# Normalising the last expert group in one batch, and the last expert's rows from its accumulators

## The chip, the cores and the metric

The kernel runs on one core of a Trainium2 chip. The core has a matrix engine (TensorE, PE in the rows, with its weight loads as PEld), a vector engine (VectorE, DVE), an activation engine (ScalarE, ACT), a general engine (GpSimd, POOL), and a queue that issues plain transfers (SyncE, SP). Every engine runs its own list of instructions in order and waits on semaphores for the others. The metric is the device time of one execution in microseconds (us). All times below are us unless ns is written.

## What is computed

One layer of a streaming encoder: two sequence mixers, a projection, and a mixture of experts, over 2048 tokens of 1024 numbers. The change is at the end, in the mixture and the last normalisation:

```python
def hier_moe(h, wg, bg, we, be, w_gate, w_up, w_down):
    """Top-1 expert group, then top-2 experts within it; gate = p(group) * softmax(top-2 logits)."""
    ...
    hg = lax.ragged_dot(xs, w_gate.astype(xs.dtype), sizes)
    hu = lax.ragged_dot(xs, w_up.astype(xs.dtype), sizes)
    ys = lax.ragged_dot(jax.nn.silu(hg) * hu, w_down.astype(xs.dtype), sizes)
    ys = ys * gates.reshape(-1)[order][:, None].astype(ys.dtype)
    y = jax.ops.segment_sum(ys, tok, num_segments=t)
    ...
        x = x + hier_moe(h2, router_g_w[layer], router_g_b[layer], router_e_w[layer], router_e_b[layer],
                         exp_w_gate[layer], exp_w_up[layer], exp_w_down[layer])
    return rmsnorm(x, norm_f_w)
```

There are 32 experts in 4 groups of 8. A token goes to one group and to two experts of it, so once the 8 experts of a group are done, the rows of all the group's tokens are final and can be normalised.

## The kernel before

The sequence mixers and the router run first, in four blocks of 512 tokens. They leave three things in device memory: the normalised tokens `x1d`, the residual rows `accd`, and lists `lst` of token numbers for each expert and each group, with their lengths in `cnt`. Then comes the expert stage, which this study is about.

**One expert.** Its tokens are gathered by number into `xg0` (the first 128) and `xg1` (those above 128, if any; when there are at most 64 of these, a form with half the rows is used, named `_half`). They are transposed on PE (`turn`) into a high part `xh` and a low part `xl`; weights are split in the same way, by a copy on ACT (`hi`, in the function `piece`) and a subtraction on DVE (`lo`). Products are summed in the accumulators `pg` and `pu` (gate and up), `act` makes the hidden rows `h` from them (Silu on ACT, a product on DVE; the half form ends with a product on POOL), `h` is transposed, and the down products land in two accumulators `pyd`, one for each half of the columns. They are copied out to `pv0` or `pv1`, and an indirect transfer adds these rows into `accd` (`puti`). Weights arrive in pieces of 512 KB into six buffers `mraw` (pool `wr_`), in the order that `stream` yields.

**The order of the work.** In this stage every engine's list is in the order in which the code is written. A string of letters sets it: step i runs through `ORDER`, each letter calls one part, and a dot feeds one more weight piece. A, B, C, D are the up products of expert i (A and C for the first 128 tokens, B and D for the rest); a and b are `act` for the two; X and Y transpose the next expert's tokens; H, K, d, e, g are the transposes of `h` and the down products of expert i-1; P and Q are its two transfers into `accd`; E and F load lists and gather tokens for expert i+2. So the down products of expert i-1 run inside step i, between its up products.

**The end of a group.** `group` assigns to each of the steps after a group's last expert a round q of that group: r (`group_count`) loads the numbers of 256 tokens into `fen` and gathers their rows from `accd` into the two tiles `f0` and `f1`, s (`group_norm`) squares and sums on ACT and takes the inverse root on POOL, m (`group_out`) scales on DVE and writes the rows to the output by number. A round is left out on the chip by a branch when the group has no tokens for it; the branch is taken on each engine, and POOL then advances the transfers' semaphores by hand. The first three groups' rounds lie inside the steps of later experts. The last group has no later experts: after step 32 its eight rounds follow one after another, lines 945 to 948.

**After the stage** comes a branch (line 952) around a slow path for lists that are too long, which these inputs don't take.

Of the kernel before, what the change touches and what calls it, by code (L numbers as in the profile page):

```python
# [38 lines left out]

ORDER = '.A.EB.HKC..r.Xa..D.b.dYePFsg..Qm'  # L40
FIRST, START = 5, 10
WB = 5
# [7 lines left out]
def hybrid_block_kernel(ctx, tc, x, norm1_w, w_in, ssd_conv_w, ssd_conv_b, ssd_dt_bias, ssd_a_log,  # L50
# [68 lines left out]

    cnt = consts.tile([1, 2 * NL + 1], I32, name="cnt")  # L120

# [336 lines left out]
    def route(b, r):  # L458
# [77 lines left out]
        if b == nblk - 1:  # L536
            pc = sc([1, NL], "pcnt")
            PE.matmul(pc, ones[:, 0:1], ohs, start=True, stop=True)
            V.tensor_scalar(cnt[:, 0:NL], pc, 63.0, None, op0=OP.add)
            V.tensor_scalar(cnt[:, NL:2 * NL], pc, 127.0, None, op0=OP.add)  # L540
            V.tensor_reduce(cnt[:, 2 * NL:], cnt[:, NL:NL + NE], axis=mybir.AxisListType.X, op=OP.max)
            V.tensor_scalar(cnt[:, 0:NL], cnt[:, 0:NL], 6, None, op0=OP.arith_shift_right)
            V.tensor_scalar(cnt[:, NL:], cnt[:, NL:], 7, None, op0=OP.arith_shift_right)
        return (last, lexp), en, sl

# [37 lines left out]
    def moe(x1, rs):  # L583

        me = ExitStack()
        wr_ = me.enter_context(tc.tile_pool(name="m_raw", bufs=RAW, reuse_waits="tile"))
# [145 lines left out]

        def down(t, h, w, n):
# [12 lines left out]

        def norm(r, sq):

            v = mp.tile([128, 2], F32, name="v")
            V.tensor_scalar(v, sq, 1.0 / D, EPS, op0=OP.mult, op1=OP.add)  # L752
            whole(rsqrt_steps(mp, r, v, 2, True))

# [86 lines left out]

        def scale_rows(t):
            V.scalar_tensor_tensor(fs[t], fs[t], r[:, t:t + 1], nf, op0=OP.mult, op1=OP.mult)

        def group_out(g, q):
            with tc.If(ngs[g] > 2 * q):
                for t in range(2):
                    scale_rows(t)
                    d = G.indirect_dma_start(out=out, out_offset=bass.IndirectOffsetOnAxis(ap=fen[t][:, 0:1], axis=0),  # L849
                                             in_=fs[t], in_offset=None, bounds_check=S - 1, oob_is_err=False)  # L850
                    apart(d, outs)
                    outs.append(d)
# [7 lines left out]
        def group_count(i):  # L860
# [4 lines left out]
            group_rows(g, q)  # L865

        def parts(i):

# [4 lines left out]
            w, wd = [], []  # L873
            fin = 0 <= group(i)[0] < NG - 1

# [28 lines left out]
            def downer(n):  # L904
                wd.extend(pull_down())
                down(0, ht[j][0], wd[4 * n:], n)

            def down_second():
                def full():
                    for n in range(2):  # L910
                        down(1, ht[j][1], wd[4 * n:4 * n + 4], n)

                def half():
                    for n in range(2):
                        down_half(ht[j][1], wd[4 * n:4 * n + 4], n)
                whole_or_half(j, full, half)

            def put1():
# [12 lines left out]
                P=(late, lambda: puti(j, 0)), Q=(late, put1), r=(fin, lambda: group_count(i)),  # L931
                s=(fin, lambda: group_norm(*group(i))), m=(fin, lambda: group_out(*group(i))))
# [12 lines left out]
        for i in range(NE + 2, NE + 2 + GE):  # L945
            group_count(i)
            group_norm(*group(i))
            group_out(*group(i))
        order.close()

        nmax = nc.values_load(cnt[0:1, 2 * NL:2 * NL + 1], min_val=0, max_val=S // 128)
        with tc.If(nmax > 2):
            for e in range(NE):
# [16 lines left out]
            with tc.For_i(0, S // 128, 1) as t:  # L970
                nc.sync.dma_start(fs[0], accd[bass.ds(t * 128, 128), :])
                square(fs[0], sq[:, 0:1])
                norm(r, sq)
                scale_rows(0)
                nc.sync.dma_start(out[bass.ds(t * 128, 128), :], fs[0])
# [326 lines left out]
```

## Time and profile before

| | us |
|---|---|
| median of 3 runs | 3080.14 |
| lowest and highest | 3077.07, 3081.48 |
| the profiled execution, its own time | 3078.34 |
| its span, first to last instruction | 3076.6 |
| TensorE busy | 2815.0 |
| VectorE busy | 2123.6 |
| ScalarE busy | 1485.0 |
| GpSimd busy | 692.5 |

The profile gives each engine's busy time in the span; a busy TensorE is not one at its peak. The span leaves out 1.74 us of the execution's own time, which lie around it. The granted clock is the share of TensorE's full clock that the chip allowed, 0.5 or 1.0 of it, averaged over a stretch.

### The profile page before, as it was taken

Reading aid. Unit: us, or ns where it says so; the run is one execution under the profiler, and the core shown is the slowest. Engines: PE = TensorE matmul, PEld = TensorE weight load, DVE = VectorE, ACT = ScalarE, POOL = GpSimd, SP = SyncE. Lnnn points to the kernel's source line nnn. Section 1 sums busy time; section 2 is a strip of 40 time slices with the busy share of each in tenths; the row PEclk is TensorE's granted clock in tenths of the full one; section 3 lists DMA queues with packets and bytes.
Section 4 is the critical chain, followed back from the end, with each engine's and each line's share of the span. In section 5 each row is a group of like instructions: output and inputs, shape, how many; then the busy total and the mean of one; then the engine's idle time right before and its main releaser. Section 6 shows DMA issues by size and latency. Waiting matters only on the chain. (4 is left out here: it accounts for less than half of the span.)

```text
span 3076.6 us, 41788 instructions
## 1 busy us (share of the span) xinstructions
PE 2815.0 (91%) x13412; PEld 2213.9 (72%) x13412; DVE 2123.6 (69%) x3969; ACT 1485.0 (48%) x2323; POOL 692.5 (23%) x770
## 2 busy tenths in 40 slices
PE   7999999999999999999999999984999899999870
PEld 6778877777877777887777788773667677777650
DVE  6896486788567679647768864855877777667741
ACT  5444345445434454434445443434666666556630
POOL 1421010451000064001025210013113323313412
PEclk9999999999999999999999999996999999999995
DMA  4222222422322241332233232145998998878951
GB/s 155 59 75 91 76 83 76 152 62 72 100 83 69 75 146 55 96 96 75 64 113 107 69 92 79 50 151 198 308 323 270 294 307 285 257 241 268 320 143 55
DMA packets 234320, 437.55 MB, mean 142 GB/s; under 512 B 43796, under 2 KB 43872, under 8 KB 234032
## 3 DMA queue, kind: packets, MB, share of 16 engines
q1 hardware_dynamic: 212064, 381.01, 38.0%
q0 software_dynamic: 21968, 53.02, 6.6%
q8 instruction: 142, 2.33, 0.3%
q14 instruction: 146, 1.20, 0.1%
HBM read 399.92 MB, written 54.98 MB: 148 GB/s over the span
## 5 line engine op out<-in xcount | busy, mean ns | idle before, releaser
L599 DVE TENSOR_TENSOR lo<-mraw,hi 128x1024 fp32r<-128x1024 f32 x384 | 456.4, 1231 | 79.3 <-ACT hi L598 64.4
L231 ACT ACTIVATE whi<-raw,pcol 128x512 fp32r<-128x512 f32 x416 | 294.9, 721 | 346.4 <-PE acc L269 143.0
L232 DVE SCALAR_TENSOR_TENSOR wlo<-raw,pcol,whi 128x512 fp32r<-128x512 f32 x416 | 317.9, 779 | 200.2 <-ACT whi L231 199.6
L598 ACT CAST hi<-mraw 128x1024 fp32r<-128x1024 f32 x384 | 384.1, 1051 | 87.0 <-DMA mraw<-in_exp_w_up_dram 39.1
L267 PE MATMUL acc<-hh,whi 128*128 128x512 f32 x896 | 366.8, 410 | 1.1 <-ACT whi L231 1.1
L267 PE MATMUL acc<-hh,wlo 128*128 128x512 f32 x896 | 358.1, 401 | 7.4 <-DVE wlo L232 7.4
L267 PE MATMUL acc<-hl,whi 128*128 128x512 f32 x896 | 361.0, 403 | 0.0
L269 PE MATMUL acc<-whi,hh 128*128 128x512 f32 x768 | 310.7, 405 | 2.0 <-ACT craw L280 2.0
L269 PE MATMUL acc<-whi,hl 128*128 128x512 f32 x768 | 310.8, 405 | 0.0
L269 PE MATMUL acc<-wlo,hh 128*128 128x512 f32 x768 | 309.4, 405 | 0.0
L269 PE MATMUL acc<-whi,mh 128*128 128x512 f32 x512 | 204.5, 399 | 0.0
L267 PEld LDWEIGHTS acc<-hh,wlo 128*128 128x128 f32 x896 | 169.3, 189 | 47.6 <-DVE wlo L232 9.8
L269 PE MATMUL acc<-whi,ml 128*128 128x512 f32 x512 | 203.5, 397 | 0.0
L269 PE MATMUL acc<-wlo,mh 128*128 128x512 f32 x512 | 203.2, 398 | 0.0
L281 POOL COPY hist<-craw 128x3 f32<-128x3 f32 x112 | 40.2, 359 | 723.7 <-ACT craw L280 723.3
L267 PEld LDWEIGHTS acc<-hh,whi 128*128 128x128 f32 x896 | 170.0, 190 | 34.4 <-issue 3.1
L267 PEld LDWEIGHTS acc<-hl,whi 128*128 128x128 f32 x896 | 169.8, 190 | 34.1 <-issue 4.6
L279 POOL COPY craw<-hist 128x3 f32<-128x3 f32 x112 | 71.0, 637 | 481.6 <-DVE ir L418 363.7
L269 PEld LDWEIGHTS acc<-wlo,hh 128*128 128x128 f32 x768 | 145.9, 190 | 36.6 <-issue 3.9
L269 PEld LDWEIGHTS acc<-whi,hh 128*128 128x128 f32 x768 | 146.1, 190 | 35.3 <-ACT craw L280 3.8
L269 PEld LDWEIGHTS acc<-whi,hl 128*128 128x128 f32 x768 | 146.1, 190 | 32.6 <-issue 1.9
L756 POOL DMA_INDIRECT accd<-pv,en x48 | 89.2, 1858 | 355.0 <-ACT hi L598 108.4
(379 smaller groups left out, 6143.6 us busy)
## 6 DMA issues: line engine op xcount, KB each, us to landing
raw<-in_w_in_dram SPq DMA_DIRECT2D x208, 512.0 KB
mraw<-in_exp_w_gate_dram SPq DMA_DIRECT2D x128, 512.0 KB
mraw<-in_exp_w_up_dram SPq DMA_DIRECT2D x128, 512.0 KB
mraw<-in_exp_w_down_dram SPq DMA_DIRECT2D x128, 512.0 KB
raw<-in_w_out_dram SPq DMA_DIRECT2D x64, 512.0 KB
xi<-in_x_dram SPq DMA_DIRECT2D x16, 512.0 KB
x<-in_x_dram SPq DMA_DIRECT2D x4, 2048.0 KB
accd<-x SPq DMA_DIRECT2D x16, 512.0 KB
```

Of the source, the lines that this page charges most:

```text
L231: A.activation(hi, src, AF.Copy, scale=w)
L232: V.scalar_tensor_tensor(lo, src, w, hi.bitcast(F32), op0=OP.mult, op1=OP.subtract)
L267: mm = PE.matmul(acc[i], b[:, s], a, start=f, stop=e)
L269: mm = PE.matmul(acc[i], a[:, s], b, start=f, stop=e)
L279: G.tensor_copy(raw[:, 0:3], hist[:, ct, :])
L281: h = G.tensor_copy(hist[:, ct, :], raw[:, T:T + 3])
L598: A.copy(hi, raw)
L599: V.tensor_tensor(lo, raw, hi.bitcast(F32), op=OP.subtract)
L756: return G.indirect_dma_start(out=accd, out_offset=bass.IndirectOffsetOnAxis(ap=en[:, 0:1], axis=0), in_=pvs[t], in_offset=None, bounds_ch ...
```

## The change

- The last two steps have strings of their own, `LAST`. In step 31, expert 30's down products come first and expert 31's up products behind them; `stream` yields the weights in that order.
- The last group is no longer handled in rounds behind step 32. In step 31, behind expert 30's transfers into `accd`, t (`last_rows`) gathers the group's first two tiles of rows and the rows of expert 31's own tokens (into `xg0` and `xg1`, which are free by then); u (`last_norm`) gathers four more tiles into weight buffers, squares all six on ACT, and takes the inverse roots of all six in one run of small instructions on DVE. In step 32, v, w and x scale two tiles each and write them out.
- Expert 31's rows no longer go through `accd`: `down` and `down_half` add the gathered rows when they empty the accumulators, and p and q (`expert_out`) square, normalise, scale and write these rows. Each write that may hit a row that an earlier one wrote waits for it.
- Rounds 4 to 7 of the first three groups are no longer there, not even as branches. Longer lists are left to the slow path, whose condition covers them.

```diff
 ORDER = '.A.EB.HKC..r.Xa..D.b.dYePFsg..Qm'
+LAST = '.H.Kd.e.PgQ.tA..B..C..ua.D.b', 'HvKwdepxgq'
+NQ = 4
...
             for i, e in enumerate(seq):
+                if i == NE - 2:
+                    yield from down_pieces(e)
+                    yield from up_pieces(seq[i + 1])
+                    continue
...
-        def down_half(h, w, n):
+        def down_half(h, w, n, g=None):
...
             A.copy(pv, pys[n][64:128])
+            if g is not None:
+                V.tensor_tensor(pv, pv, g[0:64, n * T:n * T + T], op=OP.add)
             V.tensor_tensor(pv, pys[n][0:64], pv, op=OP.add)
...
-            if n == 0:
+            if g is not None:
+                V.tensor_tensor(pv, pys[n], g[:, n * T:n * T + T], op=OP.add)
+            elif n == 0:
                 A.copy(pv, pys[n])
...
+        def last_rows():
+            for t in range(2):
+                fl.append(fs[t])
+                last_gather(fl[t], enl[:, t, :])
+            for t in range(2):
+                gt.append(xgs[t])
+                last_gather(gt[t], ens[NE - 1][t])
+
+        def last_norm():
+            assert next(rest, None) is None
+            n = 2 * NQ - 2
+            for t in range(2, n):
+                fl.append(wr_.tile([128, D], F32, name="mraw", tag="mraw"))
+                last_gather(fl[t], enl[:, t, :])
+            for t in range(n):
+                square(fl[t], sql[:, t:t + 1])
+            norm(rl[:, 0:n], sql[:, 0:n], False)
+
+        def last_out(ts):
+            for t in ts:
+                scale_rows(fl[t], fl[t], rl[:, t:t + 1])
+                d = to_out(fl[t], enl[:, t, 0:1])
+                apart(d, outs)
+                outs.append(d)
...
+        def expert_out(t):
+
+            square(pvs[t], sq[:, t:t + 1])
+            norm(r[:, t:t + 1], sq[:, t:t + 1], False)
+            scale_rows(gt[t], pvs[t], r[:, t:t + 1])
+            to_out(gt[t], ens[NE - 1][t][:, 0:1])
...
-            fin = 0 <= group(i)[0] < NG - 1
+            fin = 0 <= group(i)[0] < NG - 1 and group(i)[1] < NQ
+            rows = (lambda t: gt[t]) if j == NE - 1 else lambda t: None
...
-            for c in ORDER:
+            if i == NE - 2:
+                last_entries()
+            for c in ORDER if i < NE - 1 else LAST[i - NE + 1]:
...
-        for i in range(NE + 2, NE + 2 + GE):
-            group_count(i)
-            group_norm(*group(i))
-            group_out(*group(i))
...
-        nmax = nc.values_load(cnt[0:1, 2 * NL:2 * NL + 1], min_val=0, max_val=S // 128)
-        with tc.If(nmax > 2):
+        more_flag = nc.values_load(cnt[0:1, 2 * NL + 1:2 * NL + 2], min_val=0, max_val=S // 128 + 2 * NQ)
+        with tc.If(more_flag > 2 * NQ):
```

**ScalarE in step 31, around `act` of expert 31.** Before, the Silu that writes `h` from `pg` stands behind the last weight copies:

```order
L598 CAST hi<-mraw 128x1024 x2
L830 COMPARE_AND_BRANCH
L830 UNCONDITIONAL_BRANCH x2
L598 CAST hi<-mraw 128x1024
L732 ACTIVATE h<-pg_18244,en 128x512
L877 COMPARE_AND_BRANCH
```

and with the change:

```order
L606 CAST hi<-mraw 128x1024 x2
L962 COMPARE_AND_BRANCH
L963 COMPARE_AND_BRANCH
L963 UNCONDITIONAL_BRANCH x2
L962 UNCONDITIONAL_BRANCH
L763 ACTIVATE o,sql<-f_18244 128x1024
L763 ACTIVATE o,sql<-f_18245 128x1024
L763 ACTIVATE o,sql<-mraw 128x1024 x4
L746 ACTIVATE h<-pg_18246,en 128x512
```

The six squares now stand ahead of that Silu on its engine.

**GpSimd, from the last transfers into `accd` that the gathers wait for.** Before, that is behind expert 31 (line 663 is the gather, 837 opens `group_norm`):

```order
L863 TENSOR_LOAD cnt
L830 COMPARE_AND_BRANCH
L663 DMA f_18242<-accd,fen_31921 128x1024
L663 DMA f_18243<-accd,fen_31923 128x1024
L830 UNCONDITIONAL_BRANCH
L830 ISA
L830 UNCONDITIONAL_BRANCH
L837 COMPARE_AND_BRANCH
```

and with the change, behind expert 30 (line 675 is the gather):

```order
L675 DMA f_18244<-accd,enl 128x1024
L675 DMA f_18245<-accd,enl 128x1024
L675 DMA xg_18240<-accd,en 128x1024
L675 DMA xg_18241<-accd,en 128x1024
L962 COMPARE_AND_BRANCH
L963 COMPARE_AND_BRANCH
L963 UNCONDITIONAL_BRANCH x2
L962 UNCONDITIONAL_BRANCH
L675 DMA mraw<-accd,enl 128x1024 x4
```

Eight gathers follow one another with only the branch of B between them; before, each pair stood in a round with its norm and its writes behind it.

**VectorE in step 32, from the low part of `h`** (`hl`) **on.** Before (line 743 copies an accumulator out; 752 and 186 belong to a round):

```order
L229 TENSOR_TENSOR hl<-mt,hh 128x512
L877 COMPARE_AND_BRANCH
L878 COMPARE_AND_BRANCH
L229 TENSOR_TENSOR hh<-mt,hh 128x4x64
L878 UNCONDITIONAL_BRANCH
L229 TENSOR_TENSOR hl<-mt,hh 128x512
L878 UNCONDITIONAL_BRANCH
L877 UNCONDITIONAL_BRANCH
L830 COMPARE_AND_BRANCH
L830 UNCONDITIONAL_BRANCH x2
L743 COPY pv_18240<-pyd_18249 128x512
```

and with the change:

```order
L232 TENSOR_TENSOR hl<-mt,hh 128x512
L860 SCALAR_TENSOR_TENSOR f_18244<-f_18244,rl,nf 128x1024
L860 SCALAR_TENSOR_TENSOR f_18245<-f_18245,rl,nf 128x1024
L962 COMPARE_AND_BRANCH
L963 COMPARE_AND_BRANCH
L232 TENSOR_TENSOR hh<-mt,hh 128x4x64
L963 UNCONDITIONAL_BRANCH
L232 TENSOR_TENSOR hl<-mt,hh 128x512
L963 UNCONDITIONAL_BRANCH
L962 UNCONDITIONAL_BRANCH
L860 SCALAR_TENSOR_TENSOR mraw<-mraw,rl,nf 128x1024 x2
L755 TENSOR_TENSOR pv_18242<-pyd_18250,xg_18240 128x512
```

Four scalings of group rows now stand between the low part of `h` and the first emptied accumulator, and the emptying is an addition on VectorE where ScalarE copied.

## Rows read from the trace of the kernel before

**Rows 1.** Stretches: start:end, us; busy per engine (count); granted clock, DMA share, GB/s.

```profile
2600.00:2700.00 100.00, 99.33 (x464) 77.01 (x462) 67.92 (x76) 57.65 (x79) 28.34 (x30) 1.00 0.87 275
2986.00:3077.00 91.00, 0.00 (x0) 0.00 (x0) 9.14 (x13) 7.33 (x13) 23.24 (x49) 0.52 0.22 62
```

**Rows 2.** Timeline, all engines, from the last product: start, length, engine, line, instruction.

```profile
2985.42 0.40 PE L698 MATMUL pyd<-hi,hh 128*128 128x512 f32 x1
...
2988.00 1.56 POOL L756 DMA_INDIRECT accd<-pv,en  x1 [2.81 <-DVEq L846]
...
2995.18 1.06 POOL L663 DMA_INDIRECT f<-accd,fen  x1 [5.62 <-issue]
2996.55 1.02 POOL L663 DMA_INDIRECT f<-accd,fen  x1 [0.30 <-issue]
3000.36 1.06 ACT L747 ACTIVATE o<-f 128x1024 f32<-128x1024 f32 x1 [13.93 <-DMA f<-accd,fen]
...
3006.87 2.48 DVE L843 SCALAR_TENSOR_TENSOR f<-f,r,nf 128x1024 f32<-128x1024 f32 x2 [3.42 <-POOL r L195]
3008.43 1.83 POOL L849 DMA_INDIRECT out_dram<-f,fen  x1 [1.60 <-DVE f L843]
...
3013.56 1.04 POOL L663 DMA_INDIRECT f<-accd,fen  x1 [1.98 <-DMA out_dram<-f,fen]
...
3046.96 1.00 POOL L849 DMA_INDIRECT out_dram<-f,fen  x1 [0.31 <-DVEq L846]
```

**Rows 3.** GpSimd's queue at the end, by line: count, ns, first and last start.

```profile
L846 POOLq INC_SWDGE_SEM  x2: 1487/1489/1491, 3060.0 to 3063.8; - x2
...
L951 POOLq TENSOR_LOAD <-cnt x1: 310/310/310, 3065.3 to 3065.3; - x1
```

**Rows 4.** Timeline of TensorE in steps 31 and 32: A, d, H, d again.

```profile
2945.04 0.50 PE L686 MATMUL pg<-hi,xh 128*128 128x512 f32 x1 [0.73 <-ACT hi L598]
...
2964.80 0.40 PE L686 MATMUL pyd<-hi,hh 128*128 128x512 f32 x1
...
2974.11 0.60 PE L676 MATMUL mt<-ident,h 128*128 128x128 f32 x4
...
2976.51 0.50 PE L686 MATMUL pyd<-hi,hl 128*128 128x512 f32 x1 [0.45 <-DVE hl L229]
```

**Rows 5.** Timeline of VectorE in step 31.

```profile
2945.58 2.36 DVE L599 TENSOR_TENSOR lo<-mraw,hi 128x1024 fp32r<-128x1024 f32 x2 [0.53 <-DVEq L877]
2948.17 3.50 DVE L599 TENSOR_TENSOR lo<-mraw,hi 128x1024 fp32r<-128x1024 f32 x3 [0.23 <-DVEq L846]
2955.71 0.69 DVE L229 TENSOR_TENSOR hl<-mt,hh 128x512 fp32r<-128x512 f32 x1 [4.05 <-ACT hh L228]
...
2961.36 0.75 DVE L733 SCALAR_TENSOR_TENSOR h<-pu,en,h 128x512 f32<-128x512 f32 x1 [0.92 <-ACT h L732]
2965.19 0.68 DVE L711 TENSOR_TENSOR h<-pg,h 64x512 f32<-64x512 f32 x1 [3.09 <-ACT h L709]
```

**Rows 6.** Timeline of GpSimd in step 31: the last product of the half form.

```profile
2966.78 1.28 POOL L714 TENSOR_TENSOR h<-u,h 64x512 f32<-64x512 f32 x1 [18.52 <-ACT h L713]
```

**Rows 7.** Timeline of VectorE in a mixer stage: the inverse root's small instructions.

```profile
398.11 0.17 DVE L198 TENSOR_TENSOR rs_t<-rs_i 128x16 f32<-128x16 f32 x1
398.31 0.17 DVE L200 SCALAR_TENSOR_TENSOR rs_t<-rs_t,va 128x16 f32<-128x16 f32 x1
```

**Rows 8.** Timeline of TensorE in step 29, after an idle stretch.

```profile
2903.81 1.97 PE L676 MATMUL mt<-ident,xg 128*128 128x128 f32 x8 [4.35 <-DVE hl L229]
...
2907.67 0.63 PE L686 MATMUL pyd<-hi,hh 128*128 128x512 f32 x1
...
2908.60 0.40 PE L686 MATMUL pyd<-hi,hh 128*128 128x512 f32 x1
```

**Rows 9.** DMA issues by line: count, median us to landing.

```profile
accd<-pv,en POOLq DMA_INDIRECT x3, 8.9
...
out_dram<-f,fen POOLq DMA_INDIRECT x6, 3.4
```

More of the change, by code (lines that the diff above doesn't have):

```diff
@@ L118, in hybrid_block_kernel @@
     V.memset(ohs, 0.0)
-    cnt = consts.tile([1, 2 * NL + 1], I32, name="cnt")
+    cnt = consts.tile([1, 2 * NL + 2], I32, name="cnt")
     pcol = consts.tile([128, 172], F32, name="pcol")
@@ L733, in act, with down @@
             V.scalar_tensor_tensor(h, pas[t][1], ef[:, 4:5], h, op0=OP.mult, op1=OP.mult)
-        def down(t, h, w, n):
+        def down(t, h, w, n, g=None):
             for f, ww in enumerate(w):
@@ L747, in square, with norm @@
             A.activation(o, f, AF.Square, accum_out=sq)
-        def norm(r, sq):
-            v = mp.tile([128, 2], F32, name="v")
+        def norm(r, sq, pool_engine=True):
+            n = sq.shape[1]
+            v = mp.tile([128, n], F32, name="v%d" % n)
             V.tensor_scalar(v, sq, 1.0 / D, EPS, op0=OP.mult, op1=OP.add)
-            whole(rsqrt_steps(mp, r, v, 2, True))
+            whole(rsqrt_steps(mp, r, v, n, pool_engine))
         def add(t, en):
@@ L840, in group_norm, with scale_rows, to_out @@
                 norm(r, sq)
-        def scale_rows(t):
-            V.scalar_tensor_tensor(fs[t], fs[t], r[:, t:t + 1], nf, op0=OP.mult, op1=OP.mult)
+        def scale_rows(o, f, r):
+            V.scalar_tensor_tensor(o, f, r, nf, op0=OP.mult, op1=OP.mult)
+        def to_out(f, at):
+            return G.indirect_dma_start(out=out, out_offset=bass.IndirectOffsetOnAxis(ap=at, axis=0),
+                                        in_=f, in_offset=None, bounds_check=S - 1, oob_is_err=False)
         def group_out(g, q):
@@ L847, in group_out @@
                 for t in range(2):
-                    scale_rows(t)
-                    d = G.indirect_dma_start(out=out, out_offset=bass.IndirectOffsetOnAxis(ap=fen[t][:, 0:1], axis=0),
-                                             in_=fs[t], in_offset=None, bounds_check=S - 1, oob_is_err=False)
+                    scale_rows(fs[t], fs[t], r[:, t:t + 1])
+                    d = to_out(fs[t], fen[t][:, 0:1])
                     apart(d, outs)
@@ L865, in group_count, with last_entries, last_gather, last_more @@
             group_rows(g, q)
+        gl = NG - 1
+        sql, rl = (mp.tile([128, 2 * NQ], F32, name=n, bufs=1) for n in ("sql", "rl"))
+        enl = mp.tile([128, 2 * NQ, 8], I32, name="enl", bufs=1)
+        fl, gt = [], []
+        def last_entries():
+            at = (NE + gl) * S
+            after(nc.sync.dma_start(enl, lst[at:at + 2 * NQ * 128, :].rearrange("(t p) w -> p t w", p=128)), scat)
+        def last_gather(dst, at):
+            d = gather(dst, accd, at)
+            apart(d, [o for j, o in puts if j // GE != gl])
+        def last_rows():
[20 more added lines that the diff above has]
+                outs.append(d)
+        def last_more():
+            n = 2 * NQ - 2
+            ng = nc.values_load(cnt[0:1, NL + NE + gl:NL + NE + gl + 1], engines=ENGS, min_val=0, max_val=S // 128)
+            with tc.If(ng > n):
+                for t in range(2):
+                    last_gather(fs[t], enl[:, n + t, :])
+                    square(fs[t], sql[:, n + t:n + t + 1])
+                norm(r, sql[:, n:n + 2], False)
+                for t in range(2):
+                    scale_rows(fs[t], fs[t], r[:, t:t + 1])
+                    d = to_out(fs[t], enl[:, n + t, 0:1])
+                    apart(d, outs)
+        def expert_out(t):
[3 more added lines that the diff above has]
+            to_out(gt[t], ens[NE - 1][t][:, 0:1])
+        def expert_out1():
+            with tc.If(ns[NE - 1] > 2):
+                expert_out(1)
         def parts(i):
@@ L905, in downer @@
                 wd.extend(pull_down())
-                down(0, ht[j][0], wd[4 * n:], n)
+                down(0, ht[j][0], wd[4 * n:], n, rows(0))
             def down_second():
@@ L910, in full @@
                     for n in range(2):
-                        down(1, ht[j][1], wd[4 * n:4 * n + 4], n)
+                        down(1, ht[j][1], wd[4 * n:4 * n + 4], n, rows(1))
                 def half():
                     for n in range(2):
-                        down_half(ht[j][1], wd[4 * n:4 * n + 4], n)
+                        down_half(ht[j][1], wd[4 * n:4 * n + 4], n, rows(1))
                 whole_or_half(j, full, half)
@@ L931, in parts @@
                 P=(late, lambda: puti(j, 0)), Q=(late, put1), r=(fin, lambda: group_count(i)),
-                s=(fin, lambda: group_norm(*group(i))), m=(fin, lambda: group_out(*group(i))))
+                s=(fin, lambda: group_norm(*group(i))), m=(fin, lambda: group_out(*group(i))), t=(True, last_rows), u=(True, last_norm),
+                v=(True, lambda: last_out((0, 1))), w=(True, lambda: last_out((2, 3))),
+                x=(True, lambda: (last_out((4, 5)), last_more())), p=(True, lambda: expert_out(0)),
+                q=(True, expert_out1))
         held = 0
@@ L944, in moe @@
                     held += {"A": 4, "C": 4, "d": 2, "e": 2, "B": -4, "D": -4, "g": -4}.get(c, 0)
-        for i in range(NE + 2, NE + 2 + GE):
-            group_count(i)
-            group_norm(*group(i))
-            group_out(*group(i))
         order.close()
-        nmax = nc.values_load(cnt[0:1, 2 * NL:2 * NL + 1], min_val=0, max_val=S // 128)
-        with tc.If(nmax > 2):
+        more_flag = nc.values_load(cnt[0:1, 2 * NL + 1:2 * NL + 2], min_val=0, max_val=S // 128 + 2 * NQ)
+        with tc.If(more_flag > 2 * NQ):
+            for t in range(2):
+                G.indirect_dma_start(out=accd, out_offset=bass.IndirectOffsetOnAxis(ap=ens[NE - 1][t][:, 0:1], axis=0),
+                                     in_=pvs[t], in_offset=None, bounds_check=S - 1, oob_is_err=False)
             for e in range(NE):
@@ L973, in moe @@
                 norm(r, sq)
-                scale_rows(0)
+                scale_rows(fs[0], fs[0], r[:, 0:1])
                 nc.sync.dma_start(out[bass.ds(t * 128, 128), :], fs[0])
```

5 lines of the change are left out of this document (4 added, 1 removed).

## The prediction

> **What bounds the kernel now.** I read the stretches first, then the timeline from the last product on, then each engine's timeline in the last two steps. In a stretch of 100 us of the expert stage TensorE is busy for 99.33 [rows 1]: there the products set the time. From 2986 on TensorE does nothing for 91 us, and no other engine is busy for more than 23 of them [rows 1]. So the tail is a chain of waits, and the change is worth what it does to that chain, less what it adds ahead of it.
>
> The chain of the tail is plain in the timeline [rows 2]. The last product ends at 2985.42 + 0.40 = 2985.82. GpSimd's last transfer into `accd` follows at 2988.00, the first gather at 2995.18, 9.36 after the last product: the gather waits for that transfer to land. The gathers of a round are issued 1.37 apart. The first square starts 5.18 after its gather (2995.18 to 3000.36): the data have to land. Then come the norm on GpSimd, the scaling (2.48 for two tiles) and two writes, and the next round's gather stands at 3013.56, so a round takes 18.4. With 5 tiles of tokens three rounds run; the last write of the third is issued at 3046.96. The five empty rounds are skipped, with two semaphore advances of 1.49 on GpSimd in each, and only then is the flag of the slow path loaded, at 3065.3 [rows 3]. From there to the end of the span (3076.6) it is 11.3, which the change leaves alone.
>
> **The change part by part: step 31.** Before, A of expert 31 starts at 2945.04 after a wait of 0.73, so the products of the step ahead end at 2944.3. A to D, with H and K of expert 30 between them, run from there to d at 2964.80, and d, e and g from 2964.80 to H of expert 31 at 2974.11: 9.3 [rows 4]. Of the first stretch's 19.8 I give 1.0 to H and K (eight transposes at most, by the row of four at 2974.11 that takes 0.60), which leaves 18.8 for A to D.
>
> With the change H, K and d of expert 30 come first, so d needs `hl` at once. On VectorE that subtraction stands behind weights' low parts: the three that stand ahead of it take, as before, two from 2945.58 on and one from 2948.17 on, at 3.50 / 3 = 1.17 each, to 2949.3; `hl` itself takes 0.69: 2950.0 [rows 5]. TensorE thus waits from 2944.3 to 2950.0, where A used to cover it. The cover is gone, and this is a real cost; its lower bound is nothing, if VectorE has the low parts done sooner.
>
> A wait of that size also costs speed. After an idle stretch of 4.35 a product takes 0.63 until 2907.67, and 0.40 from 2908.60 on [rows 8]; over the 4.1 us from 2903.81 this is 4.1 x (1 - 0.40 / 0.63) = 1.5 at most, and nothing if the wait is short. I take 1.2, since some of that stretch is transposes with waits of their own. So g of expert 30 ends at 2950.0 + 9.3 + 1.2 = 2960.5, or 2960.3, since d's first products don't need `hl`. A to D add 18.8: TensorE is through at 2979.1, where before it came to H at 2974.1: 5.0 later.
>
> **The batch.** Expert 30's last transfer lands as expert 31's did: the first gather is at 2960.3 + 9.36 = 2969.7. Eight gathers at 1.37 put the eighth issue at 2979.3; its data land 5.2 later, at 2984.5, and the last square (1.06 [rows 2], and 0.1 for its sum) ends at 2985.7. The two ends of the landing are 5.2, and 8.9 as the transfers into `accd` have it [rows 9]; I take 5.2, which is a gather of the same form and size, but eight at once are asked beside what is left of the weights, and the upper end stays in the range (+3.7).
>
> Here is the price. The squares stand ahead of expert 31's Silu on ScalarE, and the batch's norm ahead of its product on VectorE. The norm is 11 small instructions 0.20 apart [rows 7], with 0.2 to hand over 2.4: 2988.1. The product of `act` takes 0.75 [rows 5], so H starts at 2989.0, and TensorE, through at 2979.1, waits 9.9. Queued behind it are K, d, e and g of expert 31, and the whole end waits for them.
>
> The Trainium skill, page "DMA: Bandwidth & Descriptors", section "Anatomy of one DMA — SWDGE (gpsimd) path", gives a fixed cost of about 2.0 us and the bytes at 436e3 a microsecond, for 512 KB an estimate of 3.2. By it the last square and H would be 2 sooner and the sum 3030; the row shows 5.2 from issue to use, and I stay with the row.
>
> **Expert 31's end.** The half form's chain runs from VectorE's instruction at 2965.19 [rows 5] to the end of GpSimd's at 2966.78 + 1.28 = 2968.06 [rows 6], 2.87: from 2988.9 to 2991.8. K and the way to d take 1.0: before, 2974.11 to the second product of d at 2976.51 held H, K and a wait of 0.45 for `hl` [rows 4], of which `hl` and H are now done beside the wait. d starts at 2992.8. d, e and g are 40 products, d and e 24 of them: 9.3 x 24 / 40 = 5.6, and 1.2 for the restart: 2999.6.
>
> Then the rows go from the accumulators, and the transfer, its 9.36 and the rounds are gone. The emptying is one addition of 0.7 behind the last product (by the row of `hl`, the same shape): 3000.4. Square 1.3: 3001.7. Norm 2.4: 3004.1. Scaling 2.48 / 2 = 1.3: 3005.4. VectorE then has two scalings of the batch's last tiles, 2.5: 3007.9, and behind them what the second accumulators need, four additions of 0.68 (the 64-row row at 2965.19 [rows 5]) and a hand-over of 0.3: 3010.9. TensorE has g done at about 3003.3 (16 products more), so this is VectorE's bound. Square 1.3, norm 2.4, scaling 1.3, with hand-overs rounded in: 3015.9. GpSimd's write is issued in 1.83 beside VectorE or about 1.0 alone [rows 2]; it ends at 3017.5. Loading the flag comes at 3017.8, and the 11.3 of before bring the span to 3029.1.
>
> GpSimd has a chain of its own: each write that may meet an earlier one's rows waits until it has landed, 3.4 from issue [rows 9]. The first four group writes go out while d and e run, the write of `xg0` waits for them, the last two group writes wait for that, and that of `xg1` for all. By these figures it is ready 1 to 3 before VectorE is: hidden, but close; if it loses, it costs up to 3.
>
> What is not counted: rounds 4 to 7 of three groups, 12 skips of about 3.8 on GpSimd each (3060.0 to 3063.8 is one [rows 3]), lie beside products, and GpSimd is busy for 28 of 100 there [rows 1]. They may be worth 0 to 3. The four added scalings of v and w (1.3 each) lie in TensorE's wait for K and in d and e; were that cover gone, they would cost 5.
>
> **The sum.** The execution before took 3078.34 with a span of 3076.6, so 1.74 lie outside. 3029.1 + 1.74 = 3030.8, 47.5 below; that execution was 1.8 below the median of 3080.14, so I predict 3080.14 - 47.5 = 3032 in round numbers. In terms: from the last product to the flag it was 3065.3 - 2985.8 = 79.5; now g ends at 2999.6 + 9.3 x 16 / 40 = 3003.3 and the flag is loaded 14.5 later, 65.0 less. Against it the last product comes 17.5 later: 5.0 and 9.9 for TensorE's two waits, and 2.6 for h's second half and the restart (H to the last product 14.3, before 11.7).
>
> **The rivals.** The waits bite less: `hl` is done when d wants it, and the gathers come faster. For it speaks that VectorE has slack (68 of 100 in the stage) [rows 1]. Then d starts at 2945.3 and g ends at 2954.6; the first gather is at 2964.0, the eighth at 2973.6, its square ends at 2980.0, 5.7 sooner than above, but D ends at 2973.4 too, so 6.6 of the second wait stay. The time would be 3026. If the gathers follow at their own length of 1.04 [rows 2], the eighth is 2.3 sooner, and 3024; with the data in a little sooner as well, about 3022. Chance 0.17.
>
> Slower gathers and writes: data after 8.9 instead of 5.2, restarts at 1.5, GpSimd's writes in front at the end: 3032 + 3.7 + 0.6 + 3 to 6, about 3041 and up to 3047. For it: eight gathers at once, where the trace has two. Chance 0.19.
>
> Slower than before: if each gather of eight had to wait for the one ahead to land, at the 8.9 of [rows 9], they would take 71 where I count 14.8 (9.6 of issue and 5.2), and the time would be 3032 + 56 = 3088. It decides from (14.8 + 48) / 8 = 7.9 each. Against it stands the pitch of 1.37 within a round [rows 2]. Chance 0.02.
>
> The change doesn't do what it says: the condition of the slow path now covers the group's list, and if it were true for these inputs, the path would run over all tokens. With 5 tiles against 8 it is not. Chance 0.01, far above 3100.
>
> **The numbers.** The forecast has 0.61, between 3026 and 3038. The range goes from 3018, with the first wait gone and the second halved, to 3047; what is left out on both sides is less than 0.2. A difference under about 0.2%, 6 us, can't be told from none here. Faster by more holds in all but the last two rivals: 0.97; same 0.01; slower 0.02.
>
> **What would show it.** In step 31 TensorE should wait some 5 for `hl` ahead of d of expert 30, and some 10 ahead of H of expert 31, released by VectorE's product, which itself waits for the norm and that for the last square. Between the last product and the flag some 15 should be left, and VectorE should hold it through x's scalings and the second accumulators' additions; a GpSimd write that waits for a landing there would show the second chain in front. Skipped rounds should be gone at the end. Wrong would be: gathers more than 2 apart, squares that don't wait, or a weight stream that is late for A after the reordering, which would show as TensorE waits for `hi` or `lo`.

## The result, and the profile after

The changed kernel takes 3029.57 us (median of 4 runs, 3028.81 to 3032.05), the kernel before in the same comparison 3078.61: a ratio of 0.9841, with a 95% interval from 0.9824 to 0.9858, so 44 to 54 us less. The prediction was 3032. The profiled execution takes 3030.05, its span is 3028.2.

TensorE in steps 31 and 32, in the timeline (columns as in [rows 4]):

```profile
2943.22 0.63 PE L688 MATMUL mt<-ident,h 128*128 128x128 f32 x4 [0.57 <-DVE xh L232]
...
2945.28 0.73 PE L698 MATMUL pyd<-hi,hh 128*128 128x512 f32 x1 [1.05 <-ACT hh L231]
2947.74 0.80 PE L698 MATMUL pyd<-hi,hl 128*128 128x512 f32 x1 [1.73 <-DVE hl L232]
...
2959.31 0.40 PE L698 MATMUL pg<-hi,xh 128*128 128x512 f32 x1
...
2977.72 0.40 PE L710 MATMUL pu<-hi,xh 128*128 128x512 f32 x1
2988.73 1.11 PE L688 MATMUL mt<-ident,h 128*128 128x128 f32 x4 [10.62 <-DVE h L747]
```

Both waits of the prediction are there: d of expert 30 waits for `hl` (the products before it ended at 2943.22 - 0.57 = 2942.65, `hl` lets it go on at 2947.74), and H of expert 31 waits 10.62 for VectorE. A to D stand between them in one run of 18.8, from 2959.31 to 2978.12.

What H waits for, and the end of the chain, all engines:

```profile
2962.00 1.74 POOL L773 DMA_INDIRECT accd<-pv,en  x1 [2.12 <-ACT hi L606]
2969.36 1.07 POOL L675 DMA_INDIRECT f<-accd,enl  x1 [5.62 <-DMA accd<-pv,en]
...
2978.57 1.00 POOL L675 DMA_INDIRECT mraw<-accd,enl  x1 [0.30 <-issue]
2984.50 1.06 ACT L763 ACTIVATE o<-mraw 128x1024 f32<-128x1024 f32 x1
2985.68 0.17 DVE L769 TENSOR_SCALAR v<-sql 128x6 f32<-128x6 f32 x1 [22.24 <-ACT o L763]
2987.93 0.75 DVE L747 SCALAR_TENSOR_TENSOR h<-pu,en,h 128x512 f32<-128x512 f32 x1
...
2999.97 0.69 DVE L755 TENSOR_TENSOR pv<-pyd,xg 128x512 f32<-128x512 f32 x1 [2.06 <-PE pyd L698]
3000.75 1.06 ACT L763 ACTIVATE o<-pv 128x1024 f32<-128x1024 f32 x1 [8.19 <-DVE pv L755]
3005.41 2.48 DVE L860 SCALAR_TENSOR_TENSOR mraw<-mraw,rl,nf 128x1024 f32<-128x1024 f32 x2
3008.25 0.68 DVE L741 TENSOR_TENSOR pv<-pv,xg 64x512 f32<-64x512 f32 x1 [0.36 <-DVEq L930]
3011.94 0.98 POOL L863 DMA_INDIRECT out_dram<-mraw,enl  x1 [0.30 <-issue]
3014.53 1.28 DVE L860 SCALAR_TENSOR_TENSOR xg<-pv,r,nf 128x1024 f32<-128x1024 f32 x1
3016.09 0.97 POOL L863 DMA_INDIRECT out_dram<-xg,en  x1 [3.17 <-DVE xg L860]
```

Read downwards: expert 30's last transfer, eight gathers to 2978.57, six squares (the last to 2985.65), the norm, the product of `act`, then H. At the end VectorE is busy from x's scalings (3005.41) on, with one gap of 1.3 for the square of the second rows, and the last write waits for its last scaling. The skipped rounds of [rows 3] are gone; the flag of the slow path is loaded right there (GpSimd's queue, by line, columns as in [rows 3]):

```profile
L1037 POOLq TENSOR_LOAD <-cnt x1: 288/288/288, 3016.0 to 3016.0; - x1
```

### The profile page after: what moved, and what is told of

Its sections match the earlier page's. It is cut to its first block, busy times and chain, and to the rows that moved or that the text cites. A ratio compares the mean times of both kernels' runs of the same rounds, so it can differ in the third digit from the quotient of the medians.

```text
span 3028.2 us, 41261 instructions
## 1 busy us (share of the span) xinstructions
PE 2820.4 (93%) x13412; PEld 2218.4 (73%) x13412; DVE 2130.8 (70%) x4003; ACT 1485.8 (49%) x2326; POOL 685.2 (23%) x736
```

## The experiments

Up to H of expert 30 on TensorE, the changed kernel and the variants that keep its order are nearly the same program; still H starts at 2943.22 in the changed kernel's profile and between 2935.44 (experiment 6) and 2944.89 (experiment 11) in theirs. Differences of a few us are therefore read as distances inside step 31 and behind it. In the changed kernel it is 18.8 from H to the last transfer into `accd` (2943.22 to 2962.00), 54.1 from there to the last write (3016.09), 72.9 in all.

**1. Squares and norm behind e.** What is H's wait worth? A letter n takes the squares and the norm out of u:

```diff
-LAST = '.H.Kd.e.PgQ.tA..B..C..ua.D.b', 'HvKwdepxgq'
+LAST = '.H.Kd.e.PgQ.tA..B..C..ua.D.b', 'HKdenvwxpgq'
```

> The six squares and the batch's norm stand in step 32 behind e instead of ahead of expert 31's Silu; the gathers stay where they are. If TensorE's wait of 10.6 ahead of H is what the batch costs, H starts at about 2978, the squares still end at 2985.7, and VectorE then sets the end: norm 2988.1, four scalings to 2993, the first rows' norm and scaling to 2997, two scalings to 2999, additions to 3002, square, norm and scaling to 3007, where it was 3015.8: about 9 less, 3021. Rival: the writes that wait for one another's landing set the end, and the wait of TensorE is hidden; the first write is then only 3.4 sooner than now, so 3026. Second rival: the wait was harmless because the squares themselves set everything behind them: 3030.

Measured 3024.28, ratio 0.9834 (0.9817 to 0.9851). Timeline, TensorE, ScalarE, VectorE and GpSimd by turns:

```profile
2976.89 0.60 PE L688 MATMUL mt<-ident,h 128*128 128x128 f32 x4
2982.34 0.68 PE L732 MATMUL mt<-ident,h 64*128 64x64 f32 x4 [4.86 <-POOL h L726]
2983.37 1.06 ACT L763 ACTIVATE o<-f 128x1024 f32<-128x1024 f32 x1
...
2989.28 1.06 ACT L763 ACTIVATE o<-mraw 128x1024 f32<-128x1024 f32 x1
2990.05 0.69 DVE L755 TENSOR_TENSOR pv<-pyd,xg 128x512 f32<-128x512 f32 x1 [2.05 <-PE pyd L698]
2990.66 0.16 DVE L769 TENSOR_SCALAR v<-sql 128x6 f32<-128x6 f32 x1
...
3011.79 0.97 POOL L863 DMA_INDIRECT out_dram<-xg,en  x1 [3.16 <-DVE xg L860]
```

H waits no more, but K, right behind it, waits 4.86 for the half form's last product on GpSimd (1.63 with the change), and the end comes only 3.7 sooner from H of expert 30 (69.2), not 9. Expert 31's first rows are emptied at 2990.74, 9.3 sooner from H of expert 30. The norm starts right there, at 2990.66, on VectorE; the six squares, in one row of 7.1 behind the copies of H and K on ScalarE, are through just before, at 2990.43. So the norm (2.3) and v's and w's four scalings (4.9), which with the change lay in the waits for H and K and beside d and e, now stand behind e: 7.2 of the 9.3 go there, and 1.6 come back, most of it since the square of the first rows now lies beside them. The wait was a cover for this work of VectorE's as much as for the squares.

**2. Only the empty rounds.** The kernel before with rounds 4 to 7 left out for every group, which these inputs have no tokens for:

```diff
-            fin = 0 <= group(i)[0] < NG - 1
+            fin = 0 <= group(i)[0] < NG - 1 and group(i)[1] < 4
-        for i in range(NE + 2, NE + 2 + GE):
+        for i in range(NE + 2, NE + 2 + 4):
```

> The kernel before with rounds 4 to 7 left out for all four groups, nothing else. If an empty round at the end costs the 3.75 that two semaphore advances and the branches take on GpSimd, and the twelve in the stage lie beside products, four of them are 15 less: 3063 to 3064, down to 3061 if the stage gains too. Rival: the last write's landing (3.4 from issue) hides part of them: 3067. Second rival: the empty rounds in the stage cost TensorE something too, about 1 each: 3052.

Measured 3056.53, ratio 0.9935 (0.9916 to 0.9954): 14 to 26 less. GpSimd's last write, and its queue's load of the flag:

```profile
3042.33 1.00 POOL L849 DMA_INDIRECT out_dram<-f,fen  x1 [0.31 <-issue]
```
```profile
L951 POOLq TENSOR_LOAD <-cnt x1: 306/306/306, 3045.0 to 3045.0; - x1
```

From write to flag it was 18.3 [rows 2, 3] and is 2.7: 15.6 for four rounds, 3.9 each, as the terms have it. The other 4 or 5 lie ahead of the write, and in the profiled executions 3.6 of them ahead of the expert stage, whose first product is at 2114.4 here and at 2118.0 before, so they are not the rounds'.

**3. The batch behind step 32.** Steps 31 and 32 and the weights in the old order, expert 31's rows through `accd`:

```diff
+LAST = ORDER, ORDER
...
-                if i == NE - 2:
-                    yield from down_pieces(e)
-                    yield from up_pieces(seq[i + 1])
-                    continue
...
+        last_rows()
+        last_norm()
+        last_out(range(6))
+        last_more()
```

> The changed kernel with steps 31 and 32 in the order and with the weights' order of before, expert 31's rows added into accd as before, and the batch of six tiles behind step 32: gathers, squares, norm and writes in one run. By the terms of the prediction: first gather at 2995.2 as before, the sixth at 3002.0, its data at 3007.2, square 3008.4, norm 3010.8, six scalings 7.5 to 3018.3, last write to 3019.7, then the flag and 11.3: span 3031, time 3033. So the batch and the missing rounds alone would give all but 3 of the change's 48, and the overlap would pay back in TensorE's waits nearly all that it saves. Rival: the gain comes from work beside the last expert's products and rows from its accumulators, and batching alone gives little more than the missing empty rounds: 3055 to 3063.

Measured 3031.33, ratio 0.9857 (0.9841 to 0.9874). GpSimd's first gather, VectorE's norm and GpSimd's last write:

```profile
2991.65 1.07 POOL L671 DMA_INDIRECT f<-accd,enl  x1 [4.39 <-DMA accd<-pv,en]
...
3005.62 0.17 DVE L765 TENSOR_SCALAR v<-sql 128x6 f32<-128x6 f32 x1 [20.77 <-ACTq L923]
...
3018.96 0.98 POOL L859 DMA_INDIRECT out_dram<-mraw,enl  x1 [0.30 <-DVEq L1035]
```

From the first gather to the last write it is 27.3 where the terms had 24.5 (data took longer, and the first writes 2 each beside scalings), and the gather came 3.5 sooner than assumed. The batch and the missing rounds alone give 45 of the 49 us, some 16 to 20 of them by the missing rounds (experiment 2); laying the batch beside expert 31's products and taking its rows from the accumulators gives what is left, and the two intervals overlap. What these two are worth one by one was not tried.

**4. Rounds 4 to 7 of the first three groups put back.**

```diff
-            fin = 0 <= group(i)[0] < NG - 1 and group(i)[1] < NQ
+            fin = 0 <= group(i)[0] < NG - 1
```

> The changed kernel with rounds 4 to 7 of the first three groups put back (twelve that are skipped by a branch). If they lie beside products, they cost 0 to 3: 3030 to 3033. Rival: each of twelve costs every engine a branch of 0.5 to 1 that nothing hides: 3036 to 3042.

Measured 3029.80, ratio 0.9857 (0.984 to 0.9874), beside 0.9841 with the change. No cost shows: from the stage's first product to H of expert 30 it is 825.1 here, and 822.4 to 827.4 in the changed kernel and the variants that keep its order. A cost below that scatter can't be excluded.

**5. Two squares early, one norm for expert 31's two tiles.** o squares the first two tiles, y is `expert_out` for both tiles with one norm. A third edit, which the expectation doesn't name: g stands ahead of the group's scalings instead of behind them.

```diff
+LAST = '.H.Kd.e.PgQ.tA..B..C..uao.D.b', 'HKdengvwxy'
```

> Like the first experiment, with two more edits: the squares of the first two tiles stand behind expert 31's first Silu, where ScalarE waits, and expert 31's two tiles of rows share one norm behind the group's writes (one run of 11 small instructions, one square out of the way). In the first experiment six squares stood in a row of 7.1 behind H and K's copies, so that the norm ended at 2993.0; with four of them it ends 2.4 sooner, and one norm and one square less are 2.2 more: the end 4 to 5 sooner than in the first experiment, 3019 to 3020. Rival: the two last writes wait for the landing of the group's last one, which comes no sooner: 3023.

Measured 3032.72, ratio 0.9864 (0.9848 to 0.988): slower than experiment 1, not faster. GpSimd's writes:

```profile
2994.06 6.60 POOL L863 DMA_INDIRECT out_dram<-f,enl  x1 [15.31 <-DVE f L860]
...
3006.46 0.98 POOL L863 DMA_INDIRECT out_dram<-mraw,enl  x1 [0.30 <-issue]
3010.99 0.97 POOL L863 DMA_INDIRECT out_dram<-xg,en  x1 [3.56 <-DMA out_dram<-mraw,enl]
3015.08 0.97 POOL L863 DMA_INDIRECT out_dram<-xg,en  x1 [3.12 <-issue]
```

The norm again starts right behind VectorE's second addition (at 2987.22), while the squares were through at 2984.3: moving two of them gained nothing. g's four additions (2.9) then stand ahead of the scalings. VectorE is through at 3005.2, but the last two writes wait for a landing each, and the first took 6.60. The rival's place was right, its size too small.

**6. TensorE kept busy ahead of H.** 42 products of no use, into an accumulator that d overwrites:

```diff
+            def warm():
+                for k in range(14):
+                    passes(pys[0], xs[i][0], k % KD, w[0], True, True)
...
+LAST = '.H.Kd.e.PgQ.tA..B..C..ua.D.zb', 'HvKwdepxgq'
```

> The changed kernel with 42 products of no use (into an accumulator that is overwritten by d) on TensorE between D and H of expert 31, 9.7 of the wait of 10.6. If the slow start of d is due to the idle stretch ahead of it, d's products stand 0.23 apart from the first on instead of 0.43 for ten of them: from H to the emptied first accumulators 2.0 sooner, and so the end of the span, since VectorE follows: 3027.5, a difference that shows in the trace and not in the median. Rival: the products are slow because gathers and products share something else: nothing changes, 3029.5.

Measured 3024.10 (2 runs), ratio 0.9834 (0.9814 to 0.9854). Stretches, columns as in [rows 1]; H is at 2981.05, K at 2983.80, d from 2984.28 on:

```profile
2980.00:2984.00 4.00, 0.88 (x8) 0.63 (x8) 3.23 (x7) 1.31 (x2) 1.26 (x1) 1.00 0.00 0
2984.00:2988.00 4.00, 4.00 (x14) 3.12 (x13) 4.00 (x5) 0.37 (x1) 2.54 (x2) 0.57 0.12 48
```

The granted clock still falls to 0.57 under d, behind the waits at H (1.0) and K (2.1) alone: seven of d's products 0.43 apart instead of ten. So 0.8 was gained by it from H to the last write (26.6, with the change 27.4), not 2.0; the rest of the 8.4 by which this profiled execution is shorter lies ahead (the last transfer into `accd` is at 2954.11 here, at 2962.00 with the change).

**7. Step 31 in the old order,** the gathers behind it, squares and norms as in experiment 5:

```diff
+LAST = '.A..B.HKC...a..D.b.d.e.P.g.Q.tu', 'HKdegonvwxy'
```

> The letters of step 31 in the old order (A, B, H, K, C ahead of d, e, g) with the weights' order of before; the gathers follow behind expert 30's transfers; squares, norms and writes stand in step 32 behind d, e and g, and the two tiles of expert 31 share a norm. TensorE doesn't wait for hl, and through g of expert 31 it runs as before, to 2986; but the first gather comes only at 2974.1 + 9.4 = 2983.5, the eighth at 2992.7, its data 6 later at 2998.7, the norm at 3002, six scalings to 3010, the second norm and two scalings to 3015, the last write near 3017: as fast as the changed kernel, 3030, and 10 behind the version with d first. Rival: the early d is worth nothing, since what it saves is paid in waits, and this is as fast as that version: 3020.

Measured 3037.02, ratio 0.9877 (0.986 to 0.9893). The first gather is at 2979.30, and TensorE, which was expected to run through, waits 10.40 ahead of g, since VectorE can't empty d's accumulators before expert 31's rows are gathered:

```profile
2988.25 0.77 PE L706 MATMUL pyd<-hi,hh 128*128 128x512 f32 x1 [10.40 <-DVE pv L751]
```

The last write follows at 3023.35, 7.1 behind VectorE's last scaling, behind two landings as in experiment 5. Without these it would be the 3030 that was expected, so what the early d is worth can't be read from this run.

**8. The last write without its wait for the other.**

```diff
-                to_out(gt[1], ens[NE - 1][1][:, 0:1])
+                apart(to_out(gt[1], ens[NE - 1][1][:, 0:1]), [d])
```

> The fifth experiment with one edit: the last write (expert 31's second tile) doesn't wait for the landing of the one ahead, whose rows are other tokens'. There the last three steps were the group's last write at 3006.5, 4.5 to the next, 4.1 to the last, while VectorE was through at 3005.2. If waits for landings set its end, the last 4.1 become 1.3: 2.8 sooner than the fifth experiment, from expert 30's last transfer to the last write 52.7 instead of 55.5, time 3030. Rival: VectorE or something else holds the last write, and nothing changes: 3032.7. Besides: the group's first write took 6.60 on GpSimd there, and about 1.8 in the other runs; if it is this order of work, it comes again.

Measured 3031.68, ratio 0.9853 (0.9835 to 0.987): 1 below experiment 5, less than can be told.

```profile
2996.79 6.60 POOL L863 DMA_INDIRECT out_dram<-f,enl  x1 [16.46 <-DVE f L860]
...
3009.18 0.98 POOL L863 DMA_INDIRECT out_dram<-mraw,enl  x1 [0.30 <-issue]
3014.32 0.97 POOL L863 DMA_INDIRECT out_dram<-xg,en  x1 [4.16 <-DMA out_dram<-mraw,enl]
3015.60 0.98 POOL L863 DMA_INDIRECT out_dram<-xg,en  x1 [0.30 <-issue]
```

The 4.1 did become 1.3, and the 6.60 came again to the hundredth; what was gained behind it was lost ahead: the batch's norm started 31.3 after expert 30's last transfer (2958.59 to 2989.93) instead of 27.7, behind a K that waits 5.3 instead of 2.7 (see experiment 12), and the first of the last two writes came 5.1 after the group's last instead of 4.5.

**9. g behind the six scalings.**

```diff
+LAST = '.H.Kd.e.PgQ.tA..B..C..uao.D.b', 'HKdenvwxgy'
```

> The eighth experiment with g behind the group's six scalings instead of ahead, so that VectorE scales from the end of the batch's norm on: the writes start some 3 sooner, the additions of expert 31's second tile and the norm of its two tiles follow. Norm 2989.5, six scalings to 2996.9, additions 2999.7, square, one norm and two scalings to 3005.7; the group's last write at about 3000.5 lands at 3004; the last write at 3006. From expert 30's last transfer to the last write 46 to 47, where the changed kernel has 54.1: 7 to 8 sooner, 3022. Rival: writes on GpSimd take 2 each beside scalings, the last of the group lands only at 3007, and 3025 comes out.

Measured 3024.32, ratio 0.9831 (0.9815 to 0.9847). The first write takes 1.81 here, the next two 2.05 and 2.07, and the last stands at 3009.58, 51.4 behind the transfer: 2.7 sooner than the changed kernel, not 7 to 8. The writes do take 2 each beside scalings, as the rival had it, but the last two wait for VectorE again; the batch's norm came 3.7 later than assumed, behind TensorE's e and the additions (K waits 5.0, where experiment 5 had 2.7), and the whole chain with it.

**10. Products of no use on both sides of H.**

```diff
+LAST = '.H.Kd.e.PgQ.tA..B..C..ua.D.zb', 'HvZKwdepxgq'
```

> The sixth experiment with 9 more products of no use between H and K, and 45 ahead of H. There the 42 kept TensorE busy until 1.0 ahead of H, and seven of d's products still came 0.43 apart, behind two waits of 1.0 and 2.1. If these waits and the transposes between them are what slows the clock, d's products now stand 0.23 apart from the first on, and from K to the emptied first accumulators it is 7.0 instead of 7.7 (8.5 in the changed kernel). Rival: the clock falls for another reason: 7.7 again.

One run, 3028.95. Stretches of it, then TensorE's timeline from K on:

```profile
2988.00:2992.00 4.00, 3.29 (x18) 2.47 (x19) 3.26 (x5) 1.34 (x3) 1.29 (x1) 1.00 0.00 0
2992.00:2996.00 4.00, 4.00 (x18) 3.28 (x19) 4.00 (x5) 0.34 (x1) 2.90 (x2) 1.00 0.21 87
```
```profile
2991.47 0.46 PE L732 MATMUL mt<-ident,h 64*128 64x64 f32 x4
2991.86 0.51 PE L698 MATMUL pyd<-hi,hh 128*128 128x512 f32 x1
2992.21 0.40 PE L698 MATMUL pyd<-hi,hl 128*128 128x512 f32 x1
```

The clock stays at 1.00, and d's products stand 0.23 apart from the second on. From K to VectorE's addition of e's columns it is 2991.47 to 2997.69, 6.2 (expected 7.0), where the changed kernel has 8.5: the slow start costs 2.3, and it is TensorE's idle time around H and K that brings it. The end gains less. VectorE's last scaling is done 24.8 after H, 2.3 sooner than with the change, but the last write is only 1.4 sooner (26.0 after H), since it now waits for the landing of the group's last write:

```profile
3014.64 0.97 POOL L863 DMA_INDIRECT out_dram<-xg,en  x1 [3.07 <-DMA out_dram<-mraw,enl]
```

**11. Weights fed behind H and K of expert 30.**

```diff
+            for c in ORDER if i < NE - 2 else ORDER.replace('g..', 'g') if i < NE - 1 else LAST[i - NE + 1]:
...
+LAST = 'HK....d.e.PgQ.tA..B..C..ua.D.b', 'HvKwdepxgq'
```

> The changed kernel with the last two weight pieces of step 30 and the first two of step 31 fed behind H and K of expert 30 instead of around H. Then hh and hl of expert 30 don't stand behind four copies on ScalarE and four low parts on VectorE: the second product of d of expert 30, which came 4.5 after H started, comes 1.6 to 2 after it. If that wait is the price of the early d, from H of expert 30 to the last transfer into accd it is some 3 less than 18.8, and everything behind it 3 sooner: 3026.5. Rival: the low parts that are moved are needed by d's own later products, which then wait in its place: 18.8 again or more, 3030.

Measured 3025.27, ratio 0.9827 (0.9812 to 0.9842). TensorE's H and d, then GpSimd's transfer and last write:

```profile
2944.89 0.63 PE L688 MATMUL mt<-ident,h 128*128 128x128 f32 x4 [0.57 <-DVE xh L232]
...
2946.92 0.50 PE L698 MATMUL pyd<-hi,hl 128*128 128x512 f32 x1 [0.23 <-DVE hl L232]
...
2960.22 1.74 POOL L773 DMA_INDIRECT accd<-pv,en  x1 [2.12 <-ACT hi L606]
...
3013.47 0.97 POOL L863 DMA_INDIRECT out_dram<-xg,en  x1 [3.19 <-DVE xg L860]
```

`hl` comes 2.0 after H instead of 4.5, TensorE's clock doesn't fall (the next products are 0.40 long), and from H to the transfer it is 15.3 instead of 18.8; to the last write 68.6 instead of 72.9.

**12. Experiments 11 and 1 together.**

> The eleventh and the first experiment together: pieces fed behind H and K of expert 30, and the six squares and the norm behind e of expert 31. If the two prices are apart from one another, this is 3 below the first experiment: 3021, and from H of expert 30 to the last write 66 instead of 68 to 69 (72.9 in the changed kernel). Rival: the gathers and ScalarE's squares hold the end in the first experiment, and an earlier step 31 shows in TensorE only: 3024.

Measured 3017.07 (5 runs, 3016.20 to 3024.45), ratio 0.9812 (0.9798 to 0.9825): the lowest ratio of all, though its interval overlaps with those of experiments 1, 6, 9 and 11 and touches that of the change. H of expert 30 and the last write:

```profile
2938.56 0.63 PE L688 MATMUL mt<-ident,h 128*128 128x128 f32 x4 [0.57 <-DVE xh L232]
...
3002.73 0.97 POOL L863 DMA_INDIRECT out_dram<-xg,en  x1 [3.12 <-DVE xg L860]
```

From one to the other 64.2: 8.7 less than with the change, where the two experiments alone gave 4.3 and 3.7. The two gains add up to within 0.7. Some 2 of it are not theirs, though: K of expert 31 waits 2.7 for the half form's last product here and in experiment 5, and 4.9 to 5.3 in experiments 1, 8 and 9. Why the same code takes longer there is not shown.

## Why the prediction was right

**The sum.** Predicted for the profiled execution 3030.8, measured 3030.05, and from the first gather (2969.36, predicted 2969.7) to the last scaling (done at 3015.8, predicted 3015.9) each step lies within 1 us of its place. That it is so close is in part luck: step 30's products ended at 2942.65, 1.7 sooner than in the execution before, and 1.3 of that was there already at the expert stage's first product (2116.7 against 2118.0; 2113.0 to 2119.6 in the experiments). Counted from the end of step 30's products, the last scaling was done 73.2 later, predicted 71.6.

**The wait for `hl`.** From the end of step 30's products it was predicted to 5.7, and was 5.1; experiment 11, which takes the copies away from ahead of it, gives 2.5 of it back and has no slow start. The restart behind it was mis-sized: ten products at 0.43 instead of 0.23, 2.0, where the prediction took 1.2 and called 1.5 the most. It reckoned with the length of one product in [rows 8], 0.63 against 0.40, instead of the distance of two. Together with 0.4 lost to a wait for an accumulator (a distance of 0.59 between two products, at 2957.37) TensorE was through with A to D 35.5 after step 30's products, predicted 34.8.

**The batch.** First gather 9.9 after g (predicted 9.36), eight issues in 9.2 (9.6), the last square 16.3 after the first gather (16.0). Data took 4.5 from the first gather to its square and 6.2 from the fifth (2974.67 to 2980.84), against 5.2 taken. The Trainium skill's page "DMA: Bandwidth & Descriptors", section "Anatomy of one DMA — SWDGE (gpsimd) path", made it 3.2 as an estimate; no gather here came in that time, they landed 4.4 to 6.1 after their issue. H waited 10.6 (9.9).

**What H's wait is worth** was not told well: the prediction wrote that the whole end waits for it. Experiment 1 takes it away and gains 3.7, since VectorE's norm and four scalings then need their 7.2 behind e. The prediction had the price of the scalings: were that cover gone, they would cost 5; they cost 4.9.

**Expert 31's end.** From H to the first emptied rows 11.9, predicted 11.4, with the same restart in it: experiment 10 shows it as 2.3. VectorE holds the end to the last scaling at 3014.53, and GpSimd's second chain stands right behind it, closer than the 1 to 3 of the prediction: the group's last write was issued at 3011.94 and landed 3.0 later, and in experiments 5 and 10 a write that waits for such a landing was issued 0.8 to 0.9 behind it. The last write could thus have stood at about 3015.8; it stood at 3016.09. Experiments 5, 7 and 8 show what happens when the chain gets in front: the last write comes 7 to 10 us behind VectorE's last scaling, 0.3 with the change.

**The flag.** It was to come behind the last write, at 3017.8, with 11.3 to the end; it was loaded at 3016.0, beside the write, and 12.2 followed; from the end of the last write (3017.06) it is 11.1.

**The terms.** The skipped rounds at the end cost 3.9 each (experiment 2), those of the other groups nothing that shows (experiment 4). The sum of 65.0 saved and 17.5 lost was nearly right: from the last product to the flag 67.1 were saved, and the last product came 19.4 later, counted from the end of step 30's products. But it doesn't say which part of the change is worth what. Experiment 3 does: one batch in place of rounds, with nothing moved beside expert 31's products, ends within 2 us of the change, because what the overlap saves it pays back, mostly in TensorE's two long waits and two slow starts: in the two profiled executions it is 35.4 from the last product to the last write there and 12.5 with the change, but 40.7 and 61.0 from the end of step 30's products to the last product.

**The rivals.** Faster gathers, slower gathers and gathers that wait for one another are excluded by the pitch of 1.3 and data after 4.5 to 6.2; the slow path was not taken.

## What to carry to other kernels

When a serial tail is turned into a batch, first price the batch alone: here it gave 45 of 49 us together with the missing empty rounds, and moving it beside the last products gave hardly more, since the moved instructions stand in engine queues ahead of what the products wait for. Look in each of these queues for what is ahead of the one small instruction that TensorE needs: taking four weight copies from ahead of `hl` and six squares from ahead of a Silu gave another 8.7 us between H of expert 30 and the last write, though some 2 of them have another, unknown cause. And look at what the wait covered: work that is moved out of it has to stand somewhere else. And follow the writes that wait for one another's landing as a chain of their own, since an order that is better for VectorE can put that chain in front.

## What the runs showed of the hardware

A write by number on GpSimd takes 0.97 to issue alone, and mostly 1.8 to 2.1 beside VectorE's scalings (two inputs of 128x1024). In experiments 5 and 8 the first such write took 6.60 in each: it began in VectorE's run of six scalings and ended 0.9 behind it, and then the next took 0.99; in experiments 1 and 9, with the same six scalings in a row, it took 1.81. The Trainium skill, page "SBUF — State Buffer", section "Who interferes with whom", says that a VectorE instruction with two inputs in SBUF contends with a GpSimd instruction that reads SBUF, and that the port pair which the two share is an exclusive lock. The 1.8 to 2.1 and the 6.60 fit with it if a write by number reads SBUF on GpSimd, which no run here shows; why a write got in between two scalings in some orders and was held through six in others stays open.

TensorE's granted clock fell from 1.00 to a mean of 0.57 in the stretch from 2984 to 2988 (products first at the lower level of 0.5, then at 1.0) behind waits of only 1.0 and 2.1 with four transposes behind each (experiment 6), and stayed at 1.00 when these were filled with products but for 0.7 (experiment 10).
